# An fp32 attention block on one core: every engine's instructions in the order of the program, with sums, weight splits and weighting at other places in it

## The chip, the core and the metric

The kernel runs on one core of one Trainium2 chip. A core has five engines that each work through a list of instructions of their own: TensorE (PE, matrix products into the banks of PSUM), VectorE (DVE), ScalarE (ACT), GpSimd (POOL) and SyncE (SP, which here only issues loads). An instruction starts when the one before it on its engine has been issued and the semaphores that it waits for have been raised, so what stands ahead of it in its engine's list can hold it up, whether or not the two have anything to do with each other. The metric is the device time of one execution in microseconds (us), as the median of several runs.

## The reference

The reference is a two-layer decoder trunk in fp32 on a sequence of 512 tokens with a model width of 1024: a recurrent layer with its feed-forward block, and an attention layer with its own. The change touches the attention layer alone:

```python
def dilated_attention_mixer(h, w_q, q_norm, w_o, k, v, cos, sin):
    q = (h @ w_q).reshape(B, S, N_GROUPS, Q_HEADS, HEAD_DIM)    # 3 groups, 8 heads of 128
    q = rms_norm(q, q_norm[:, None, :])
    q = apply_partial_rope(q, cos, sin)                         # turns the first 32 of 128 elements
    q = q.reshape(B, S, N_GROUPS, KV_HEADS, Q_PER_KV, HEAD_DIM)
    for g, (window, dilation) in enumerate(DILATION_GROUPS):    # (128, 1), (512, 4), (2048, 16)
        o, l = dilated_window_attention(q[:, :, g], k[:, :, g], v[:, :, g], window, dilation)
    ...
    wts = jax.nn.softmax(jnp.stack(lses, axis=0), axis=0)       # the groups weighted by their sums
    o = jnp.sum(wts[..., None] * jnp.stack(outs, axis=0), axis=0)
    return o.reshape(B, S, Q_HEADS * HEAD_DIM) @ w_o
```

The two weightings together are one softmax over the keys of all three groups, and so the kernel computes it.

## The kernel before, in words

The activations lie transposed, as 8 blocks of 128 features by 512 tokens. A product in fp32 is made of three products in a faster format: each operand x is split into a rounded part hi and a rest lo = x - hi, and PE forms hi·hi, lo·hi and hi·lo (`mm3`, L163 to L165; in the projections L1048 to L1050).

**The weights** come in pieces of 128x1024 through `Stream` (L70 to L153): SP loads a piece into one of two raw buffers `wr`, and two pieces ahead of its use it is split into `wh` and `wl`, of which there are three buffers each. For most pieces ACT copies hi (L117) and DVE subtracts (L124). For pieces of kind "dma", those of the query and output projections among them, ACT copies hi, ACT writes the negated weight into lo (L120), and POOL issues a DMA that adds to it (L121).

**The query passes** (`project`, L1030) take one group of keys (g = 0, 1, 2) and one half of the heads (kv = 0, 1) each: 16 steps of 6 matmuls, four weight pieces by four tiles of 128 tokens. In the last piece each step completes one tile of queries for four heads, and `collect` (L971) follows it up: DVE applies the gain out of the bank (`kn`, L982), ACT squares the bank in place (L984), DVE sums the squares (L985) and rotates (`rotate`, four small operations, L994 to L997). After the last tile, `normed` gives DVE the `factors` (L1006 and eight operations of `rsqrt`, L261 to L270, some 0.2 us each) and one `scale` of a tile per step (L1014). A given number of steps later, the lag, PE transposes each tile (`turn`, L1127), and ACT copies the result out (`qt`, L1129). A call `at(n, fn)` puts such work off by n steps; `tick` counts them. `tick` comes straight after `done` in the same step, so that `at(1, ...)` falls due at once.

**The attention** (`attend`) goes through 32 units: 2 halves kv by 4 blocks n of 128 tokens by 4 phases p. For a unit u, `scores` forms three products in one bank, normally bank S, of which there is one. `softmax` then has DVE add the masks and find the least (two operations, L1192 and L1195), ACT take the exponential (L1200), DVE the reciprocal (L1201) and POOL the multiplication with it (L1202). Three units later `turned` transposes the weights (L1214) and `halve` splits them into `ph` (ACT, L279) and `pl` (DVE, L280); after every second unit, `values` multiplies them with the values. `query_parts` splits the queries of the next block n into `qh` (ACT) and `ql` (DVE), three each. At the end of the first half, `move` splits four tiles of the output `o_t` by `halve`.

**What fills the gaps.** While `attend` runs, `plan` inserts the steps of the second half's query passes (groups 0 and 1 as passes of four tiles, group 2 as an early and a late pass of two tiles) and then those of the first half of the output projection. The second half of that projection, and the second feed-forward block, follow.

**What sets the order.** In the attention, the framework's scheduler decides how the instructions of each engine are ordered: it goes by its own model of when each is ready, and takes weight splits, the softmax and the splits of `turned` first, since these stand under `high_priority`. The feed-forward blocks stand under `manual_schedule` for all five engines, which keeps the order in which the program issues.

Of the kernel before, what the change touches and what calls it, by code (L numbers as in the profile page):

```python
# [73 lines left out]
class Stream:  # L74


    def __init__(self, tc, nc, pool, pieces, ahead_load, ahead_split):
# [4 lines left out]
        self.hold, self.gate = {}, {}  # L82

# [22 lines left out]
    def _split(self, i):  # L106
# [8 lines left out]
        def do(c):  # L115
            with self.tc.high_priority():
                nc.scalar.copy(hi[:, c], r[:, c])  # L117
                kind = self.pieces[i][1]
                if kind == "dma":
                    nc.scalar.mul(lo[:, c], r[:, c], -1.0)  # L120
                    nc.gpsimd.dma_start(lo[:, c], self.pieces[i][0][:, c], accum_op=ALU.add)  # L121
                else:
# [34 lines left out]
def trunk(tc, A, out):  # L157
    nc = tc.nc
# [58 lines left out]
    p_q = add_pieces([A["w_q"][i] for i in (*range(24), *range(20, 24))], "dma")  # L217
# [725 lines left out]
def attention(tc, A, ap, ws, env):  # L943
# [30 lines left out]
    def collect(raw, nh, j, n, st, tab, g_row):  # L974
# [10 lines left out]
        V.tensor_reduce(st["sq"][:, j], rows.rearrange("q (i d) -> q i d", i=nh), mybir.AxisListType.X, ALU.add)  # L985
        st["kn"].append(dst)
        at(1, lambda: rotate(x, nh, tab))
# [11 lines left out]
    def normed(st, nh, tab, turn, lag, tiles=range(4)):  # L999
# [16 lines left out]
        at(1, factors)  # L1016
        for j, t in enumerate(tiles):
            at(2 + j, lambda t=t: scale(t))
            at(lag + j, lambda t=t: turn(t, kn[t]))
# [96 lines left out]
    def project_q(kv):  # L1116
# [3 lines left out]
        for j, (g, tiles) in enumerate(passes):  # L1120
            def done_q(t, ps, g=g, st={}, tiles=tiles, j=j):
                collect(ps, 4, t - tiles[0], len(tiles), st, t, 3 + g)
                if t == tiles[-1]:
# [10 lines left out]
                    normed(st, 4, 0, turn, {3: 7}.get(j, 8), tiles)  # L1134

            yield from project(p_q + 12 * kv + 4 * j, xh, xl, done_q, tiles)

    def first(fn):

        def run(*args):  # L1140
            with tc.high_priority():
                return fn(*args)
        return run

# [13 lines left out]
    def query_parts(kv, n):  # L1158
        for g in range(3):
            if (kv, n, g) not in qs_:  # L1160
                query_part(kv, n, g)

    def scores(kv, n, p):
# [20 lines left out]
        softmax(n, p, ps, pr, mn, g0, w, nb)  # L1184
        prs[kv, n, p] = pr
        if n < 3 and p == (2 if kv else 3) or not kv and p == 3 and (0, 1, 2) in qt:
            query_parts(kv + n // 3, (n + 1) % 4)

    @first
    def softmax(n, p, ps, pr, mn, g0, w, nb):  # L1190
# [8 lines left out]
        den = ap.tile([128, 1], F32, name="den", bufs=4)  # L1199
        S.activation(pr[:, :width], pr[:, :width], AF.Exp, bias=mn[:, 1:2], scale=-1.0, accum_out=den)  # L1200
        V.reciprocal(den, den)  # L1201
        G.tensor_scalar(pr[:, :width], pr[:, :width], den, None, ALU.mult)  # L1202
# [5 lines left out]
    def turned(kv, n, p):  # L1208
# [10 lines left out]
        first(halve)(pt.rearrange("q (b k) -> q b k", k=128)[:, :nb], ph[:, :nb, p % 2], pl[:, :nb, p % 2])  # L1219

    def values(kv, n, p):
# [23 lines left out]
        else:  # L1245
            halve(src, *(x[:, 4 * kv:4 * kv + 4, ns].rearrange("q h (p i) -> q h p i", p=4)
                         for x in (env["xhs"], env["xls"])))

    def attend():
# [3 lines left out]
        for u in range(32 + LAG):  # L1253
            if u >= LAG:
                turned(*units[u - LAG])
            yield u + 0.4
            if u < 32:
# [29 lines left out]

    drain(project_q(0))
# [96 lines left out]
```

## Time and profile before

| what | value |
|---|---|
| median of 3 runs | 1165.84 us (1165.73 to 1167.09) |
| profiled execution, its own time | 1166.22 us |
| its span in the trace | 1164.4 us |
| PE busy | 1151.9 us, 99% of the span |
| DVE busy | 851.5 us, 73% |
| ACT busy | 623.8 us, 54% |
| POOL busy | 186.3 us, 16% |

By the places of its lines in the trace, the keys and values are projected until about 577 us, the first half's query passes run until about 645, the attention with all that fills it until about 798, the rest of the output projection until 828, and the second feed-forward block to the end. A busy time counts each instruction from its start to its end as the profiler models it; instructions of one engine overlap at their ends. A matmul of 512 columns is shown as 0.39 us long, while the next one starts about 0.23 us behind it, so a PE that is 99% busy may still have waited, and the stalls have to be read from the starts and from the waits.

### The profile page before, as it was taken

The numbers are of one execution on the slowest core, as the hardware profiler recorded it, in microseconds if no ns is written. First come the engines' busy times: TensorE is split into PE (matmuls) and PEld (weight loads), VectorE is DVE, ScalarE is ACT, GpSimd is POOL, SyncE is SP. The second block draws the span as 40 slices with busy tenths as digits, with TensorE's granted clock in tenths as the row PEclk, the third lists the DMA queues.
The fourth block names the chain that finished last, engine by engine and source line by source line (L and its number), as shares of the span: only waits on it lengthen the run. The fifth ranks groups of instructions, "written<-read, shape, count | busy, mean of one in ns | idle before, by whom it ended". The sixth has DMA issues, their size and how long they took to land.

```text
span 1164.4 us, 15128 instructions
## 1 busy us (share of the span) xinstructions
PE 1151.9 (99%) x5403; PEld 952.2 (82%) x5403; DVE 851.5 (73%) x1525; ACT 623.8 (54%) x901; POOL 186.3 (16%) x221
## 2 busy tenths in 40 slices
PE   9999999999999999999999999999999999999998
PEld 6788888888888888888888888798888888888887
DVE  7988688968777676887565667765988777676864
ACT  6797455543435353565555667665555435353532
POOL 4210010201011000020411334341002011011000
PEclk9999999999999999999999999999999999999999
DMA  7643366966665723433978657534668665757323
GB/s 244 149 114 110 105 225 159 242 193 160 183 164 174 188 73 82 129 107 89 222 182 178 142 113 179 127 73 108 219 160 233 186 165 177 182 162 191 81 71 128
DMA packets 92234, 179.61 MB, mean 154 GB/s; under 512 B 8704, under 2 KB 27008, under 8 KB 92160
## 3 DMA queue, kind: packets, MB, share of 16 engines
q1 hardware_dynamic: 72720, 130.80, 34.6%
q0 software_dynamic: 18864, 47.19, 22.9%
q8 instruction: 43, 0.70, 0.2%
q10 hardware_dynamic: 576, 0.66, 0.2%
q14 instruction: 31, 0.25, 0.1%
HBM read 164.99 MB, written 2.10 MB: 143 GB/s over the span
## 4 chain that ended last, share of the span: by engine, by line
PE 92%; DVE 3%; ACT 2%; issue 1%; DMA 1%; POOL 0%; ACTq 0%; DVEq 0%; SPq 0%
PE ps L165 25%; PE ps L164 25%; PE ps L163 25%; PE ps L1048 5%; PE ps L1049 5%; PE ps L1050 5%; PE ps L1127 1%; PE ps L1214 1%; DVE xc L451 1%; DMA h<-in_x 0%; ACT pr L1200 0%; PE ps L296 0%; DVE ql L280 0%; ACT wh L117 0%; DMA wr<-in_w_in 0%
## 5 line engine op out<-in xcount | busy, mean ns | idle before, releaser
L117 ACT CAST wh<-wr 128x1024 fp32r<-128x1024 f32 (+2 forms) x136 | 131.2, 969 | 136.3 <-PE ps L164 83.1
L164 PE MATMUL ps<-wl,xh 128*128 128x512 f32 x320 | 124.7, 390 | 0.0
L165 PE MATMUL ps<-wh,xl 128*128 128x512 f32 x320 | 124.7, 390 | 0.0
L163 PE MATMUL ps<-wh,xh 128*128 128x512 f32 x320 | 124.7, 390 | 0.0
L165 PE MATMUL ps<-gh,wl 128*128 128x512 f32 x288 | 114.6, 398 | 0.3
L163 PE MATMUL ps<-gh,wh 128*128 128x512 f32 x288 | 113.8, 395 | 0.0
L164 PE MATMUL ps<-gl,wh 128*128 128x512 f32 x288 | 113.7, 395 | 0.0
L124 DVE TENSOR_TENSOR wl<-wr,wh 128x1024 fp32r<-128x1024 f32 (+2 forms) x93 | 100.0, 1083 | 17.4 <-ACT wh L117 17.0
L649 POOL DMA_DIRECT2D S<-in_f_in x40 | 48.2, 1237 | 370.8 <-DMA S<-in_f_in 187.2
L163 PE MATMUL ps<-xh,wh 128*128 128x512 f32 x256 | 101.1, 396 | 0.7 <-ACT xh L274 0.7
L663 ACT CAST wh<-S 128x1024 fp32r<-128x1024 f32 x60 | 63.0, 1050 | 70.4 <-PE ps L165 28.0
L164 PE MATMUL ps<-xl,wh 128*128 128x512 f32 x256 | 100.2, 391 | 0.1
L165 PE MATMUL ps<-xh,wl 128*128 128x512 f32 x256 | 100.0, 391 | 0.0
L664 DVE TENSOR_TENSOR wl<-S,wh 128x1024 fp32r<-128x1024 f32 x60 | 73.2, 1222 | 31.5 <-ACT wh L663 31.5
L163 PE MATMUL ps<-wh,T 128*128 128x512 f32 x240 | 93.6, 390 | 0.0
L165 PE MATMUL ps<-wh,T 128*128 128x512 f32 x240 | 93.6, 390 | 0.0
L164 PE MATMUL ps<-wl,T 128*128 128x512 f32 x240 | 93.5, 390 | 0.0
L1048 PE MATMUL ps<-wh,xh 128*128 128x512 f32 x224 | 91.6, 409 | 0.0
L1050 PE MATMUL ps<-wh,xl 128*128 128x512 f32 x224 | 87.8, 392 | 0.0
L1049 PE MATMUL ps<-wl,xh 128*128 128x512 f32 x224 | 87.4, 390 | 0.0
L781 DVE TENSOR_TENSOR h<-h,ps 128x512 f32<-128x512 f32 x64 | 43.3, 685 | 54.9 <-PE ps L165 54.9
L163 PEld LDWEIGHTS ps<-wh,xh 128*128 128x128 f32 x320 | 60.1, 188 | 12.6
(284 smaller groups left out, 2669.7 us busy)
## 6 DMA issues: line engine op xcount, KB each, us to landing
S<-in_f_in SPq DMA_DIRECT2D x40, 512.0 KB, 6.4
S<-in_f_in POOLq DMA_DIRECT2D x40, 512.0 KB, 8.9
wr<-in_f_out SPq DMA_DIRECT2D x36, 512.0 KB, 5.2
wr<-in_w_q SPq DMA_DIRECT2D x28, 512.0 KB, 6.9
wl<-in_w_q POOLq DMA_DIRECT2D x28, 512.0 KB, 7.6
GA<-in_f_in SPq DMA_DIRECT2D x20, 512.0 KB, 4.9
GB<-in_f_in SPq DMA_DIRECT2D x20, 512.0 KB, 6.9
UB<-in_f_in SPq DMA_DIRECT2D x20, 512.0 KB, 4.9
```

Of the source, the lines that this page charges most:

```text
L117: nc.scalar.copy(hi[:, c], r[:, c])
L124: a = eng.tensor_tensor(lo[:, c], r[:, c], hi[:, c].bitcast(F32), ALU.subtract)
L163: PE.matmul(ps, wh, xh, start=first, stop=False, skip_group_check=on)
L164: PE.matmul(ps, wh, xl, start=False, stop=False, skip_group_check=on)
L165: PE.matmul(ps, wl, xh, start=False, stop=last, skip_group_check=on)
L649: nc.gpsimd.dma_start(c, p.part(1, q, n == "S1", i), accum_op=ALU.add)
L663: S.copy(hi, r)
L664: V.tensor_tensor(lo, r, hi.bitcast(F32), ALU.subtract)
L781: V.tensor_tensor(by_time(x), by_time(x), in_turn(ps), ALU.subtract)
L1048: PE.matmul(ps[t], xh[k][:, r], wh[:, c], start=k == 0, stop=False)
L1049: PE.matmul(ps[t], xh[k][:, r], wl[:, c], start=False, stop=False)
L1050: PE.matmul(ps[t], xl[k][:, r], wh[:, c], start=False, stop=k == 7)
```

## The change

1. From the first query pass to the end of the first half of the output projection, all five engines stand under `manual_schedule`; the `high_priority` of softmax and of the splits in `turned` is gone.
2. In that stretch `lo_first` has ACT write the negated weight ahead of hi, so that the accumulating DMA is issued earlier, and `al` asks for raw pieces four ahead rather than two.
3. Of the first twelve query pieces every second one is split by DVE (L124) and not by the DMA.
4. The sum of squares is issued with the rotation, in `at(1, ...)`; factors and scales come one step later; the lags become 8 for passes of four tiles and 6 for those of two.
5. `weigh` (reciprocal and multiplication) and the subtractions for `pl`, and for the split of the attention's output, go into a list `put_off`, which `catch_up` empties in the next unit, just ahead of that unit's `scores`. The first group's query split is issued ahead of the exponential, the other two behind it.

```diff
+        self.lo_first = False
...
             with self.tc.high_priority():
-                nc.scalar.copy(hi[:, c], r[:, c])
                 kind = self.pieces[i][1]
+                if kind != "dma" or not self.lo_first:
+                    nc.scalar.copy(hi[:, c], r[:, c])
                 if kind == "dma":
                     nc.scalar.mul(lo[:, c], r[:, c], -1.0)
                     nc.gpsimd.dma_start(lo[:, c], self.pieces[i][0][:, c], accum_op=ALU.add)
+                    if self.lo_first:
+                        nc.scalar.copy(hi[:, c], r[:, c])
...
-    p_q = add_pieces([A["w_q"][i] for i in (*range(24), *range(20, 24))], "dma")
+    p_q = add_pieces([A["w_q"][i] for i in range(12)], "dma", 2)
+    add_pieces([A["w_q"][i] for i in (*range(12, 24), *range(20, 24))], "dma")
...
         S.activation(rows, rows, AF.Square)
-        V.tensor_reduce(st["sq"][:, j], rows.rearrange("q (i d) -> q i d", i=nh), mybir.AxisListType.X, ALU.add)
+        sums = st["sq"][:, j]
+
+        def reduce():
+            V.tensor_reduce(sums, rows.rearrange("q (i d) -> q i d", i=nh), mybir.AxisListType.X, ALU.add)
+
         st["kn"].append(dst)
-        at(1, lambda: rotate(x, nh, tab))
+        if nh == 2:
+            reduce()
+            at(1, lambda: rotate(x, nh, tab))
+        else:
+            at(1, lambda: (reduce(), rotate(x, nh, tab)))
...
-        at(1, factors)
+        wait = 1 if nh == 2 else 2
+        at(wait, factors)
         for j, t in enumerate(tiles):
-            at(2 + j, lambda t=t: scale(t))
+            at(wait + 1 + j, lambda t=t: scale(t))
             at(lag + j, lambda t=t: turn(t, kn[t]))
...
-                    normed(st, 4, 0, turn, {3: 7}.get(j, 8), tiles)
+                    normed(st, 4, 0, turn, 8 if len(tiles) == 4 else 6, tiles)
...
-        softmax(n, p, ps, pr, mn, g0, w, nb)
+        lowest(n, p, ps, pr, mn, g0, w, nb)
         prs[kv, n, p] = pr
-        if n < 3 and p == (2 if kv else 3) or not kv and p == 3 and (0, 1, 2) in qt:
-            query_parts(kv + n // 3, (n + 1) % 4)
+        groups = ()
+        if n < 3 and p == (2 if kv else 3) or not kv and n == p == 3 and (0, 1, 2) in qt:
+            groups = range(3)
+        query_parts(kv + n // 3, (n + 1) % 4, groups[:1])
+        width = g0 + 2 * w
+        den = ap.tile([128, 1], F32, name="den", bufs=4)
+        S.activation(pr[:, :width], pr[:, :width], AF.Exp, bias=mn[:, 1:2], scale=-1.0, accum_out=den)
+        query_parts(kv + n // 3, (n + 1) % 4, groups[1:])
+
+        def weigh():
+            V.reciprocal(den, den)
+            G.tensor_scalar(pr[:, :width], pr[:, :width], den, None, ALU.mult)
+
+        put_off.append(weigh)
+
+    put_off = []
+
+    def catch_up():
+        while put_off:
+            put_off.pop(0)()
...
-        first(halve)(pt.rearrange("q (b k) -> q b k", k=128)[:, :nb], ph[:, :nb, p % 2], pl[:, :nb, p % 2])
+        parts(pt.rearrange("q (b k) -> q b k", k=128)[:, :nb], ph[:, :nb, p % 2], pl[:, :nb, p % 2])
+
+    def parts(src, hi, lo):
+        S.copy(hi, src)
+        put_off.append(lambda: V.tensor_tensor(lo, src, hi.bitcast(F32), ALU.subtract))
...
             yield u + 0.4
+            catch_up()
             if u < 32:
                 scores(*units[u])
...
+    manual = tc.manual_schedule(engines={E.PE, E.DVE, E.Activation, E.SP, E.Pool})
+    manual.__enter__()
+    ws.lo_first, ws.al = True, 4
     drain(project_q(0))
...
     drain(o0)
-    ws.asp = 1
+    catch_up()
+    ws.asp, ws.al, ws.lo_first = 1, 2, False
+    manual.__exit__(None, None, None)
```

On SP the order is the same row by row. On PE the transposes of the turns stand elsewhere at four places and a few matmuls have changed places with their neighbours; DVE and ACT are reordered throughout. Three places of the program are shown. The number behind a name tells one buffer's use from the next; it differs a little between the two programs.

**DVE, the first units of the attention (kv = 0, n = 0), while the third query pass of the first half is followed up.** `ps` with `grow` is the gain of a finished tile, `ps` with `ssum` and with `far` are the two mask operations of a unit. Before, from the third tile on:

```order
L982 TENSOR_TENSOR kn_5622<-ps_5430,grow_1855 128x512
L1192 ISA pr_5642,mn_5643<-ps_5632,ssum_78 128x128
L1192 ISA mn_5643 128x1
L994 TENSOR_TENSOR ra_5626<-kn_5622,cc_1862 128x128
L1195 ISA pr_5642,mn_5643<-ps_5632,far_1853,mn_5643 128x128
L1195 ISA mn_5643 128x1
L985 TENSOR_REDUCE sqc_5571<-ps_5430 128x4
L995 TENSOR_TENSOR rbt_5627<-kn_5622,ss_1863 128x4x16
```

Now, from the third tile on:

```order
L987 TENSOR_TENSOR kn_5620<-ps_5429,grow_1855 128x512
L993 TENSOR_REDUCE sqc_5569<-ps_5429 128x4
L1007 TENSOR_TENSOR ra_5624<-kn_5620,cc_1862 128x128
L1008 TENSOR_TENSOR rbt_5625<-kn_5620,ss_1863 128x4x16
L1009 TENSOR_TENSOR rbt_5625<-kn_5620,ss_1863 128x4x16
L1010 TENSOR_TENSOR kn_5620<-ra_5624,rbt_5625 128x4x32
L1202 RECIPROCAL den_5596<-den_5596 128x1
L1215 ISA pr_5642,mn_5643<-ps_5632,ssum_78 128x128
L1215 ISA mn_5643 128x1
L1218 ISA pr_5642,mn_5643<-ps_5632,far_1853,mn_5643 128x128
```

The sum now stands directly behind the gain of its own tile, with nothing between them, the rotation behind the sum, and the mask operations of the unit behind the whole tile. Where the mask operations of unit 2 stood behind one gain, they now stand behind two whole tiles, that of the second and that of the third.

**ACT, the first tile of the second half's pass for group 1.** Before:

```order
L120 ACTIVATE wl157_5999<-wr157_5996 128x1024
L117 CAST wh157_5998<-wr157_5996 128x1024
L1200 ACTIVATE pr_5988,den_5992<-pr_5988,mn_5989 128x512
L984 ACTIVATE ps_5692<-ps_5692 128x512
L984 ACTIVATE ps_5730<-ps_5730 128x512
```

Now:

```order
L1198 ACTIVATE pr_5988,den_5992<-pr_5988,mn_5989 128x512
L122 ACTIVATE wl157_5997<-wr157_5774 128x1024
L125 CAST wh157_5996<-wr157_5774 128x1024
L989 ACTIVATE ps_5688<-ps_5688 128x512
L989 ACTIVATE ps_5727<-ps_5727 128x512
```

The two passes over a weight piece, which stood ahead of the exponential, now stand between it and the square of the first tile.

**DVE, the end of the follow-up in the same pass.** Before, the subtraction `pl` stands ahead of the factors (the row of `epsv` is their first):

```order
L997 TENSOR_TENSOR kn_6097<-ra_6101,rbt_6102 128x4x32
L280 TENSOR_TENSOR pl_6054<-ps_6119,ph_6053 128x3x128
L1201 RECIPROCAL den_6087<-den_6087 128x1
L985 TENSOR_REDUCE sqc_6009<-ps_5769 128x4
L1192 ISA pr_6150,mn_6151<-ps_6140,ssum_78 128x256
L1192 ISA mn_6151 128x1
L1006 SCALAR_TENSOR_TENSOR sqc_6009<-sqc_6009,epsv_4010 128x16
```

Now, from the first of the factors:

```order
L1019 SCALAR_TENSOR_TENSOR sqc_6007<-sqc_6007,epsv_4010 128x16
L266 TENSOR_SCALAR qr4y_6106<-sqc_6007 128x16
L269 TENSOR_TENSOR qr4a_6107<-qr4y_6106,sqc_6007 128x16
L270 SCALAR_TENSOR_TENSOR qr4a_6107<-qr4a_6107,qr4y_6106 128x16
L271 SCALAR_TENSOR_TENSOR qr4y_6106<-qr4a_6107,qr4y_6106 128x16
L272 SCALAR_TENSOR_TENSOR qr4a_6107<-qr4y_6106,sqc_6007 128x16
L273 TENSOR_TENSOR qr4a_6107<-qr4a_6107,qr4y_6106 128x16
L274 SCALAR_TENSOR_TENSOR qr4a_6107<-qr4a_6107 128x16
L275 SCALAR_TENSOR_TENSOR qr4y_6106<-qr4a_6107,qr4y_6106 128x16
L1027 TENSOR_TENSOR kn_6008<-kn_6008,qr4y_6106 128x512
L1202 RECIPROCAL den_6087<-den_6087 128x1
L1242 TENSOR_TENSOR pl_6052<-ps_6116,ph_6051 128x3x128
```

The subtraction for which `values` waits has moved behind the nine operations of the factors and one scale; before, it stood ahead of them.

More of the change, by code (lines that the diff above doesn't have):

```diff
@@ L1132, in turn @@
                             query_part(0, 0, g)
-                    normed(st, 4, 0, turn, {3: 7}.get(j, 8), tiles)
+                    normed(st, 4, 0, turn, 8 if len(tiles) == 4 else 6, tiles)
             yield from project(p_q + 12 * kv + 4 * j, xh, xl, done_q, tiles)
[L1138 to L1143, printed above, removed]
     o_t = ap.tile([128, 4, 384], F32, name="o_t", bufs=1)
@@ L1156, in query_part, with query_parts @@
         qs_[kv, n, g] = qh, ql
-    def query_parts(kv, n):
-        for g in range(3):
+    def query_parts(kv, n, groups=range(3)):
+        for g in groups:
             if (kv, n, g) not in qs_:
@@ L1183, in scores, with lowest @@
         mn = ap.tile([128, 2], F32, name="mn", bufs=4)
-        softmax(n, p, ps, pr, mn, g0, w, nb)
+        lowest(n, p, ps, pr, mn, g0, w, nb)
         prs[kv, n, p] = pr
-        if n < 3 and p == (2 if kv else 3) or not kv and p == 3 and (0, 1, 2) in qt:
-            query_parts(kv + n // 3, (n + 1) % 4)
-    @first
-    def softmax(n, p, ps, pr, mn, g0, w, nb):
+        groups = ()
[14 more added lines that the diff above has]
+            put_off.pop(0)()
+    def lowest(n, p, ps, pr, mn, g0, w, nb):
         width = g0 + 2 * w
@@ L1198, in softmax @@
             far[:, 0:2 * nb, f0:f0 + 64], 1.0, mn[:, 0:1], ALU.add, ALU.min, mn[:, 1:2])
[L1199 to L1202, printed above, removed]
     def blocks(n, p):
@@ L1245, in values @@
         else:
-            halve(src, *(x[:, 4 * kv:4 * kv + 4, ns].rearrange("q h (p i) -> q h p i", p=4)
+            parts(src, *(x[:, 4 * kv:4 * kv + 4, ns].rearrange("q h (p i) -> q h p i", p=4)
                          for x in (env["xhs"], env["xls"])))
@@ L1285, in move @@
             halve(o_t[:, i, :], xh[i][:, 0:384], xl[i][:, 0:384])
+    E = mybir.EngineType
+    manual = tc.manual_schedule(engines={E.PE, E.DVE, E.Activation, E.SP, E.Pool})
+    manual.__enter__()
+    ws.lo_first, ws.al = True, 4
     drain(project_q(0))
```

## The prediction

> **What bounds the kernel now.** I read the busy time and the chain first, then the windows of the stretch that the change covers, then what PE waits for there. On the page, busy time by engine and the chain that ended last:
>
> ```profile
> PE 1151.9 (99%) x5403; PEld 952.2 (82%) x5403; DVE 851.5 (73%) x1525; ACT 623.8 (54%) x901; POOL 186.3 (16%) x221
> PE 92%; DVE 3%; ACT 2%; issue 1%; DMA 1%; POOL 0%; ACTq 0%; DVEq 0%; SPq 0%
> ```
>
> PE is the bound, and the change takes no matmul away. It can gain only what PE waits in the stretch from 577 to 798 us, and lose whatever other engines deliver later than PE asks for it. Two windows of the attention (start:end and length; sum and busy time with counts of PE, weight load, DVE, ACT, POOL; clock, DMA share, GB/s):
>
> ```profile
> 645.00:700.00 55.00, 54.44 (x325) 47.29 (x325) 38.73 (x140) 36.20 (x66) 19.35 (x17) 1.00 0.57 128
> 700.00:735.00 35.00, 32.27 (x214) 28.33 (x213) 25.44 (x75) 27.82 (x48) 14.66 (x11) 1.00 0.77 175
> ```
>
> Here DVE is busy 70 and 73%, ACT 66 and 79%: each has room on average, but little, so that the order within a few microseconds decides. What PE waits for from 640 to 800 us (sum, count, longest):
>
> ```profile
> PE ps L1127 <- ACT qt L1129: 1.3, 2, 1.0
> PE ps L165 <- DVE ql L280: 1.3, 2, 0.7
> PE ps L163 <- ACT qt L1129: 1.2, 1, 1.2
> PE ps L163 <- DVE mn L1195: 0.5, 1, 0.5
> PE ps L164 <- DVE pl L280: 0.3, 1, 0.3
> ```
>
> That is 4.6 us, and it is the gain that is there to be had; by the gaps between matmul starts I make it at most 7. The question is what the new order makes late.
>
> **Prices.** Grouped rows of the stretch, first DVE's weight split, then sum, ACT's two weight passes, the query split and its copy out, DVE's half of it, and one of the four splits of `move` (busy, mean ns):
>
> ```profile
> L124 DVE TENSOR_TENSOR wl<-wr,wh 128x1024 fp32r<-128x1024 f32 x3 | 3.7, 1223 | 0.2 <-ACT wh L117 0.2
> L985 DVE TENSOR_REDUCE sqc<-ps 128x4 f32<-128x512 f32 x20 | 13.7, 685 | 1.1 <-ACT ps L984 1.1
> L120 ACT ACTIVATE wl<-wr 128x1024 fp32r<-128x1024 f32 x9 | 9.5, 1059 | 3.1 <-PE ps L1049 3.0
> L117 ACT CAST wh<-wr 128x1024 fp32r<-128x1024 f32 x9 | 9.3, 1034 | 0.0
> L279 ACT CAST qh<-qt 128x512 fp32r<-128x512 f32 x9 | 5.1, 619 | 1.0 <-PE ps L164 1.0
> L1129 ACT COPY qt<-ps 128x512 f32<-128x512 f32 x8 | 4.6, 578 | 3.1 <-PE ps L1127 3.0
> L280 DVE TENSOR_TENSOR ql<-qt,qh 128x512 fp32r<-128x512 f32 x9 | 6.1, 684 | 2.0 <-ACT qh L279 2.0
> L279 ACT CAST xh<-o_t 128x384 fp32r<-128x384 f32 x4 | 2.0, 513 | 0.0
> ```
>
> The sum's row tells most: 20 sums wait only 1.1 us for their squares, since DVE does other work meanwhile. The timeline shows how long a square takes, and how close operations follow each other:
>
> ```profile
> 649.42 0.69 DVE L982 TENSOR_TENSOR kn<-ps,grow 128x512 f32<-128x512 f32 x1 [2.35 <-PE ps L1050]
> 650.14 0.58 ACT L984 ACTIVATE ps<-ps 128x512 f32<-128x512 f32 x1 [0.32 <-DVE kn L982]
> 650.14 0.29 DVE L994 TENSOR_TENSOR ra<-kn,cc 128x128 f32<-128x128 f32 x1
> 650.95 0.28 DVE L1192 CUSTOM_DVE_ANT_0 pr<-ps,ssum 128x128 f32<-128x128 f32 x1
> 653.73 0.68 DVE L985 TENSOR_REDUCE sqc<-ps 128x4 f32<-128x512 f32 x1
> 654.33 0.67 DVE L982 TENSOR_TENSOR kn<-ps,grow 128x512 f32<-128x512 f32 x1
> 654.93 0.27 DVE L1192 CUSTOM_DVE_ANT_0 pr<-ps,ssum 128x128 f32<-128x128 f32 x1
> 585.52 0.17 DVE L1006 SCALAR_TENSOR_TENSOR sqc<-sqc,epsv 128x16 f32<-128x16 f32 x1
> 587.51 2.50 DVE L1014 TENSOR_TENSOR kn<-kn,qr4y 128x512 f32<-128x512 f32 x4
> 684.59 0.42 DVE L1192 CUSTOM_DVE_ANT_0 pr<-ps,ssum 128x256 f32<-128x256 f32 x1 [1.21 <-PE ps L165]
> 685.06 0.48 DVE L1195 CUSTOM_DVE_ANT_1 pr<-ps,far,mn 128x256 f32<-128x256 f32 x1
> 685.64 0.73 ACT L1200 ACTIVATE pr<-pr,mn 128x512 f32<-128x512 f32 x1 [0.38 <-DVE mn L1195]
> ```
>
> From gain to rotation stand 0.72 us, the rotation takes 0.81 (650.14 to 650.95), a sum 0.60 and a gain without a wait 0.60. The square ends at 650.72, 1.30 us after its gain began; I put the sum's start at 1.33. In the new order nothing stands between them, so a tile costs DVE 1.33 + 0.60 + 0.81 = 2.75 us, 0.73 of it waiting. If the square were always done in time it would be 2.01; that is the lower end, and the upper one has an ACT operation of 1.03 to 1.06 ahead of the square. I take 2.75, as in the row, since the square cannot start before the gain has read the bank. A tile leaves PE every 1.36 us or so (6 matmuls of 0.23). The factors take 587.51 - 585.52 = 2.0 us with a small wait, 1.9 without; a scale 0.63; the mask pair about 0.95 (684.59 to 685.54), some 0.7 for unit widths of 128.
>
> **The change part by part.** Each place is a walk along DVE's or ACT's new order from an event of before, up to the moment at which PE asked.
>
> *First half, passes 1 and 2.* The first gain, and the last matmul ahead of the turn, then the turn:
>
> ```profile
> 577.45 0.69 DVE L982 TENSOR_TENSOR kn<-ps,grow 128x512 f32<-128x512 f32 x1 [1.79 <-PE ps L1050]
> 590.65 0.40 PE L1050 MATMUL ps<-wh,xl 128*128 128x512 f32 x1
> 590.88 0.60 PE L1127 MATMUL ps<-ident,kn 128*128 128x128 f32 x4
> ```
>
> From 577.45: 0.45 for an ACT pass that holds up the first square, four tiles at 2.75, the split of a weight piece that now stands ahead of the factors (1.22), factors 1.9, first scale 0.7: 592.7, where PE asks at 590.9. That is 1.8; pass 2, with the same walk less the 0.45, 1.4; pass 3 turns inside the attention. **+3.2**. With 2.01 a tile it would be 0.
>
> *Units n = 0.* The third scores of the attention and the query split that ends a wait of 0.7:
>
> ```profile
> 656.97 0.22 PE L163 MATMUL ps<-kh,qh 128*128 128x128 f32 x1
> 661.93 0.69 DVE L280 TENSOR_TENSOR ql<-qt,qh 128x512 fp32r<-128x512 f32 x1
> ```
>
> First gain at 649.42, tile through at 652.2, mask pair of unit 1 at 652.95; then two whole tiles (5.5) and the pair of unit 2 (0.7): bank S is free at 659.15, and PE wants it for unit 3 at 656.97, 2.2 late. Behind it a fourth tile (2.75), factors (1.9), scale (0.6), reciprocal and `pl` (0.35), the pair of unit 3 (0.7): 665.4; then three `ql` of 0.6: 667.2 against 662.67 (the last of these rows and its 0.7). **+4.5**; with 2.01 a tile, 2.3.
>
> *Second half, group 1.* Scores and values of two units:
>
> ```profile
> 694.28 0.35 PE L163 MATMUL ps<-kh,qh 128*128 128x256 f32 x1
> 696.77 0.28 PE L163 MATMUL ps<-ph,vh 128*128 128x256 f32 x1
> ```
>
> ACT now does exponential (685.64 to 686.4 with its accumulator), two weight passes (2.0), square: the first sum starts at 689.0. The rest of that tile (1.4), two more (5.5), `pl` (0.5) and mask pair (0.95) end at 697.4; PE wants the bank at 694.28: 3.1. A fourth tile (2.75), factors, scale, `pl` (0.5): 703.1; PE wants that `pl` 0.1 behind 696.77 + 3.1: 3.2. The turns stand behind weight passes on ACT: 1.5 by the same walk. Sum 7.8, less what PE waits there today (the L1127 rows, and some that the waits do not list: 2.3). **+5.5**; 2.5 at 2.01 a tile.
>
> *Early pass of group 2.*
>
> ```profile
> 714.73 0.69 DVE L982 TENSOR_TENSOR kn<-ps,grow 128x512 f32<-128x512 f32 x1
> 718.75 0.28 PE L163 MATMUL ps<-kh,qh 128*128 128x256 f32 x1
> 721.14 0.28 PE L163 MATMUL ps<-ph,vh 128*128 128x256 f32 x1
> ```
>
> A tile (2.75), `pl` (0.6) and mask pair (0.95) from 714.73 and with their hand-overs end at 719.6: 0.9 late. A second tile, factors, scale, `pl`: 725.5, where PE, 0.9 late, asks at 722.1: 3.3. **+4.2**; at 2.01, 2.7.
>
> *Change of halves.* All on ACT in one row now: mask pair 0.95, exponential 0.9, weight passes 2.1, two copies out 1.2, four splits of `move` 2.05, `ph` 0.5, three `qh` 1.9, and DVE's `ql` 0.7: 10.2, with two hand-overs 10.6. PE's matmuls between the scores of the last unit and those of the next half come to 4.8 us, each taken with its usual distance to the next: 5.8, less 1.5 that it waits there today (1.2 of it listed). **+4.3**; 3 if operations overlap as elsewhere.
>
> *The rest.* The late pass of two tiles comes out even by the same walk: 2.4 against 2.3. SP's order does not change, and of raw buffers there are two, so "four ahead" is worth 0. Six accumulating DMAs less, and POOL's multiplication later, lie under POOL's 84% idle time: 0; uncovered, a later multiplication would delay the transposes three units on, some 10 us away. Past 798 us nothing differs: 0.
>
> Sum: 3.2 + 4.5 + 5.5 + 4.2 + 4.3 = 21.7. The profiled execution took 1166.2 us, 0.4 more than the median. 1166.2 + 21.7 = 1187.9, and 1187.5 against the median. With every lower end it is 0 + 2.3 + 2.5 + 2.7 + 3 = 10.5, so 1176; with an ACT pass ahead of half of the 16 tiles concerned, +8 to +12, about 1200.
>
> **Rivals.**
>
> *A, faster.* The order of the program lets every engine take what PE needs next, and the five waits go: 1161, or 1159 with what the waits do not list. For it speaks DVE's idle quarter. It needs DVE not to wait for squares: at 2.01 a tile the walks still leave 10 us, so the gains would also have to be asked for later than today. Point of decision: mask pairs end ahead of 656.97 and 694.28.
>
> *B, no change.* The stalls move from `qt` and `ql` to the mask pairs and cost what they cost today, since a PE that is delayed by 2 us asks for everything behind it 2 us later, and one stall pays for the next. I have counted so within a place; if it holds between places too, and tiles cost 2.01, it is 1165 to 1168.
>
> *C, slower still.* [...] The chip's clock is 1.00 in both windows above, where no stall is longer than 1.4 us; at the head of the program, behind idle time, matmuls of the same width run slower:
>
> ```profile
> 1.45 4.02 PE L346 MATMUL ps<-warm 128*128 128x512 bf16 x9 [1.45 <-DVE warm L343]
> ```
>
> Nine in 4.02 us are about 0.43 each, twice the 0.23 of later. If each of four stalls (3.1, 3.2, 3.3, 5.8) costs some 3.7 us at half pace, so 1.8 us each, it is 7 more: 1195. [...]
>
> **How the numbers follow.** The forecast 1187 has 0.66 (1176 to 1200 its own range), C 0.12, A 0.13, B 0.09. The range is to leave out no more than A and the top of C: 1163 to 1201. Against a measurement that tells about 0.2% (2.3 us) from no change: faster 0.13, same 0.09, slower 0.78.
>
> **What would show it.** In the profile of the changed kernel: the sum's group waits for ACT some 0.7 us in each of about 20 tiles (14 us, against 1.1); PE waits for the mask operations by 2 to 3 us at two places, for `pl` by 3 at two, for `ql` by about 5 at the change of halves; the windows lose PE time there and nowhere after 798. If sums wait but PE does not, the walks have the wrong moment at which PE asks, and the forecast falls to B. If PE's waits are each under 1 us, A holds. If the clock falls under 1.00, C does.

## The result

The changed kernel takes 1217.57 us (median of 4 runs, 1208.35 to 1218.52), the kernel before 1166.32 us beside it: a ratio of 1.0421 with an interval of 1.037 to 1.0472, so 51 us slower. The direction was forecast, the size was not: 1217.6 lies above the range of 1163 to 1201. Busy time by engine, the chain and the clock in 40 slices, from the page of the changed kernel:

```profile
PE 1177.2 (97%) x5403; PEld 968.9 (80%) x5403; DVE 860.4 (71%) x1531; ACT 616.8 (51%) x895; POOL 180.4 (15%) x215
PEclk9999999999999999999999888899999999999999
PE 85%; DVE 8%; ACT 3%; issue 2%; DMA 1%; POOL 1%; ACTq 0%; DVEq 0%; POOLq 0%
```

The matmuls are the same 5403, and DVE and ACT have 11% of the chain where they had 5%. New is the second row: the clock granted to PE falls in four slices, which it did nowhere before. Three windows of the attention (columns as in the prediction; the clock is the third number from the end):

```profile
645.00:700.00 55.00, 50.35 (x274) 42.62 (x275) 26.49 (x94) 29.53 (x54) 13.29 (x14) 0.94 0.51 115
700.00:750.00 50.00, 40.27 (x224) 34.63 (x223) 29.66 (x99) 25.71 (x44) 16.30 (x13) 0.85 0.58 127
750.00:800.00 50.00, 40.45 (x203) 34.94 (x201) 23.79 (x78) 24.62 (x49) 11.43 (x11) 0.77 0.39 85
```

From 645 to 700 us PE issues 274 matmuls where it issued 325, and it is slowed as well as idle. What PE waits for from 570 to 870 us, and the row of the sums among DVE's groups:

```profile
PE ps L168 <- DVE pl L1242: 7.5, 5, 3.1
PE ps L167 <- DVE mn L1218: 7.4, 4, 2.9
PE ps L1141 <- DVE kn L1027: 3.0, 2, 1.7
PE ps L167 <- ACT qh L284: 2.9, 1, 2.9
PE ps L168 <- DVE xl L1242: 2.9, 1, 2.9
PE ps L1063 <- DMA wl<-in_w_q: 1.7, 1, 1.7
L993 DVE TENSOR_REDUCE sqc<-ps 128x4 f32<-128x512 f32 x24 | 16.6, 692 | 19.5 <-ACT ps L989 19.5
```

The sums wait 19.5 us in 24 tiles, 0.8 each, where 20 of them waited 1.1 before. Where the long stalls lie, in the timeline of PE (start, duration, and in brackets the wait):

```profile
664.25 0.30 PE L167 MATMUL ps<-kh,qh 128*128 128x128 f32 x1 [1.92 <-DVE mn L1218]
670.47 0.55 PE L167 MATMUL ps<-kh,qh 128*128 128x256 f32 x1 [2.00 <-DVE mn L1218]
709.57 0.36 PE L167 MATMUL ps<-kh,qh 128*128 128x256 f32 x1 [2.92 <-DVE mn L1218]
715.40 0.58 PE L168 MATMUL ps<-pl,vh 128*128 128x256 f32 x1 [2.38 <-DVE pl L1242]
745.62 0.58 PE L168 MATMUL ps<-pl,vh 128*128 128x256 f32 x1 [3.15 <-DVE pl L1242]
760.94 0.33 PE L167 MATMUL ps<-kh,qh 128*128 128x128 f32 x1 [2.89 <-ACT qh L284]
787.08 0.80 PE L168 MATMUL ps<-xl,wh 128*128 128x512 f32 x1 [2.86 <-DVE xl L1242]
```

The trace's own records of the clock give the stretches at half speed (start and length in us; the end of the program left out):

```
670.43  6.83      711.39 10.24      745.53 10.24
762.59  6.83      786.49 10.24      841.10  3.41
```

All lengths are multiples of 3.41 us, and so, within 0.02, are the distances between the starts (711.39 - 670.43 is 12 times 3.413). So the decision seems to be made on a fixed grid; I call one stretch of it a cell.

**An account by starts.** For each matmul from 570 to 880 us I took the distance to the next start and subtracted the median distance for its width (0.227 us for 512 columns, 0.12 for 256, 0.11 for 128). In a stretch at half clock, up to one more such distance is put down to the clock; the rest of an excess over 0.25 us is a stall. In us, with the table's kernels explained below:

| kernel | span | stalls | clock | smaller excess | at half clock, stretches |
|---|---|---|---|---|---|
| before | 1164.4 | 6.7 | 0 | 2.8 | 0 |
| changed | 1216.6 | 37.6 | 19.5 | 4.5 | 47.8, 6 |
| changed, second trace | 1213.7 | 39.9 | 13.1 | 4.4 | 34.1, 6 |
| all edits but the fixed order | 1165.5 | 5.9 | 0 | 4.1 | 0 |
| fixed order alone | 1237.9 | 50.8 | 25.6 | 6.5 | 64.9, 12 |
| sums a step later | 1204.7 | 27.0 | 17.5 | 3.7 | 41.0, 6 |
| fixed order on PE and SP alone | 1175.4 | 11.7 | 5.5 | 3.4 | 13.7, 2 |
| fixed order on DVE, ACT, POOL alone | 1196.5 | 26.0 | 9.2 | 5.9 | 23.9, 3 |
| three repairs | 1198.8 | 25.7 | 13.2 | 4.2 | 34.1, 6 |

The span grew by 52.2 us, and the account gives 30.9 of stalls, 19.5 of clock and 1.7 of smaller excess. So there are two things to test: where the stalls come from, and whether the slow clock is a cost of its own or only lies in time that PE would wait anyway.

### The profile page after: what moved, and what is told of

It is laid out like the page before. It is cut to its first block, busy times and chain, and to the rows that moved or that the text cites. A ratio compares the mean times of both kernels' runs of the same rounds, so it can differ in the third digit from the quotient of the medians.

```text
span 1216.6 us, 15135 instructions
## 1 busy us (share of the span) xinstructions
PE 1177.2 (97%) x5403; PEld 968.9 (80%) x5403; DVE 860.4 (71%) x1531; ACT 616.8 (51%) x895; POOL 180.4 (15%) x215
## 4 chain that ended last, share of the span: by engine, by line
PE 85%; DVE 8%; ACT 3%; issue 2%; DMA 1%; POOL 1%; ACTq 0%; DVEq 0%; POOLq 0%
PE ps L169 24%; PE ps L168 24%; PE ps L167 23%; PE ps L1062 4%; PE ps L1063 4%; PE ps L1064 4%; DVE sqc L993 1%; ACT ps L989 1%; PE ps L1141 1%; ACT pr L1198 1%; DVE kn L987 1%; PE ps L1233 1%; DMA wl<-in_w_q 1%; DVE xc L456 0%; DVE pl L1242 0%
## 5 line engine op out<-in xcount | busy, mean ns | idle before, releaser
L120 ACT CAST wh<-wr 128x1024 fp32r<-128x1024 f32 (+2 forms) x109 | 103.2, 954 | 139.6 <-PE ps L168 80.1
L167 PE MATMUL ps<-wh,xh 128*128 128x512 f32 x320 | 124.5, 389 | 0.0
L128 DVE TENSOR_TENSOR wl<-wr,wh 128x1024 fp32r<-128x1024 f32 (+2 forms) x99 | 107.2, 1091 | 23.6 <-ACT wh L120 23.4
L669 DVE TENSOR_TENSOR wl<-S,wh 128x1024 fp32r<-128x1024 f32 x60 | 73.2, 1222 | 31.5 <-ACT wh L668 31.5
L1062 PE MATMUL ps<-wh,xh 128*128 128x512 f32 x224 | 94.3, 421 | 0.0
```

The lines of the kernel that those rows point to most:

```text
L128: a = eng.tensor_tensor(lo[:, c], r[:, c], hi[:, c].bitcast(F32), ALU.subtract)
L167: PE.matmul(ps, wh, xh, start=first, stop=False, skip_group_check=on)
L669: V.tensor_tensor(lo, r, hi.bitcast(F32), ALU.subtract)
L1062: PE.matmul(ps[t], xh[k][:, r], wh[:, c], start=k == 0, stop=False)
```

## The experiments

**All edits but the fixed order.**

```diff
-    manual = tc.manual_schedule(engines={E.PE, E.DVE, E.Activation, E.SP, E.Pool})
-    manual.__enter__()
...
-    manual.__exit__(None, None, None)
```

> The changed kernel with every edit but the manual schedule: the framework's scheduler orders all five engines again, from the changed program. Theory (the fixed order is what puts DVE's and ACT's work behind what it waits for): the stalls of 2 to 3 us go, and with them the stretches at half clock; 1164 to 1170. Rival (the put-off sums, weighting and splits are late in themselves, whoever orders them): PE still waits 2 us or more for mask operations, pl or xl at several places, and the time stays above 1190.

1167.56 us (10 runs), ratio 1.0009 (0.9999 to 1.0018). The longest of PE's waits:

```profile
PE ps L1141 <- ACT qt L1143: 2.1, 4, 1.0
PE ps L167 <- ACT ph L1241: 1.0, 2, 0.6
```

The theory holds. With the put-offs, the new lags, lo ahead of hi and the DVE splits in place, but the scheduler in charge, the time is that of before within what can be measured. The 51 us need the fixed order.

**The fixed order alone**, added to the kernel before by the same lines.

> The kernel before with nothing but the manual schedule added over the same stretch: nothing is put off. Theory (a fixed order alone costs, and the put-offs repair a part of it): slower than the changed kernel, 1225 to 1250, since subtractions and reciprocals then stand on DVE directly behind the ACT operation that they wait for. Rival (the put-offs are the cause): 1170 to 1195.

1239.72 us (one run). Its waits begin with

```profile
PE ps L1049 <- DMA wl<-in_w_q: 16.4, 4, 4.7
PE ps L164 <- DVE pl L280: 7.9, 5, 3.6
PE ps L163 <- DVE mn L1195: 5.6, 2, 2.9
```

The time is as the theory said: the fixed order costs 73 us on the program as it was, and the other edits win back 22 of them. The reason given there, subtractions and reciprocals behind what they wait for, is only a part of it: PE waits longest for the accumulating DMAs (16.4 us, 1.7 in the changed kernel).

**Sums a real step later.**

```diff
-            at(1, lambda: (reduce(), rotate(x, nh, tab)))
+            at(2, lambda: (reduce(), rotate(x, nh, tab)))
```

> The changed kernel with the sum and the rotation of a tile put off by one real step, so that the next tile's gain stands between a gain and its sum. Theory of the prediction (DVE's wait of 0.73 us for each square carries half of the stalls): a tile costs 2.0 us of DVE instead of 2.75, the stalls of 2.1, 2.1 and 3.1 at the mask operations shrink to under 1.5, half of the drops in the clock go; 1185 to 1200. Rival (what ACT has ahead of the squares, and pl behind the factors, carry them): 1210 to 1220, as the changed kernel.

1205.87 us (4 runs), ratio 1.0337 (1.0322 to 1.0353). The sums' row, and the longest of PE's waits:

```profile
L993 DVE TENSOR_REDUCE sqc<-ps 128x4 f32<-128x512 f32 x24 | 16.4, 683 | 3.3 <-ACT ps L989 3.3
PE ps L168 <- DVE pl L1242: 7.5, 5, 3.3
PE ps L167 <- ACT qh L284: 3.0, 2, 2.9
PE ps L168 <- DVE xl L1242: 2.9, 1, 2.9
PE ps L167 <- DVE mn L1218: 2.4, 1, 2.4
```

The mechanism is shown: one step moves the sums' wait from 19.5 to 3.3 us, PE's wait for the mask operations from 7.4 to 2.4, and the waits of the first passes' turns for `kn` (3.0) are gone from the list. The size is less than expected: 11.7 us, to 1206 and not 1200, since PE waits for `pl`, `qh` and `xl` as long as before, and all six stretches at half clock remain, where half of them were to go.

**The clock by itself.** Ten stalls in the second feed-forward block of the kernel before, where PE does not wait otherwise, made by ACT between two matmuls into one bank:

```diff
+                    if kk and p is p_f2 and n in ("S2", "UB"):
+                        for _ in range(probes.pop(0)):      # 4, 5, 6, 7, 8, 6, 7, 5, 8, 6
+                            S.copy(ps[1], ps[1])
```

> The kernel before with ten stalls put into PE's work of the second feed-forward block, where PE otherwise never waits: ACT copies a bank onto itself 4 to 8 times between two matmuls that add to it, which should hold PE up for about 1.4, 1.9, 2.4, 2.9 and 3.4 us, two stalls of each length some 16 us apart or more. Theory G (the clock is decided on a fixed grid of 3.41 us, by PE's share of work in one cell): stalls of 1.4 and 1.9 never drop the clock, 3.4 mostly does, and 2.4 and 2.9 do so or not, depending on where they fall in a cell. [...] Each drop lasts 3.4 to 10.2 us at half clock, by the changed kernel's trace, and costs up to half of that.

1219.95 us (one run). The stalls came out longer than intended. Five of them waited for 3.59 to 5.97 us, each with a whole cell in which no matmul ran, and all five dropped the clock, as theory G has it. So the other five decide, the first, second, sixth, eighth and tenth; in PE's timeline:

```profile
873.57 0.50 PE L163 MATMUL ps<-wh,T 128*128 128x512 f32 x1 [1.79 <-ACT ps L751]
899.76 0.50 PE L163 MATMUL ps<-wh,xh 128*128 128x512 f32 x1 [2.39 <-ACT ps L751]
1044.21 0.50 PE L163 MATMUL ps<-wh,xh 128*128 128x512 f32 x1 [2.99 <-ACT ps L751]
1116.04 0.50 PE L163 MATMUL ps<-wh,xh 128*128 128x512 f32 x1 [2.39 <-ACT ps L751]
1173.53 0.50 PE L163 MATMUL ps<-wh,xh 128*128 128x512 f32 x1 [2.99 <-ACT ps L751]
```

The eight stretches begin at 874.88, 926.08, 970.46, 997.76, 1045.55, 1072.86, 1117.23 and 1144.54. So a stall of 2.39 dropped the clock once and once not, one of 2.99 once and once not, and one of 1.79 did. The cells of that grid in which those five stalls lie, for the last one both over which it stretches (start:end and length, then sum and busy time of PE, and the rest as above):

```profile
871.47:874.88 3.41, 1.62 (x8) 1.10 (x7) 0.67 (x2) 2.91 (x5) 0.05 (x1) 1.00 0.88 298
895.36:898.78 3.42, 2.01 (x9) 1.32 (x8) 3.37 (x5) 3.10 (x6) 0.00 (x0) 1.00 1.10 258
1042.14:1045.55 3.41, 1.34 (x6) 1.13 (x7) 0.40 (x1) 2.88 (x5) 0.00 (x0) 1.00 0.25 95
1113.82:1117.23 3.41, 1.19 (x5) 1.02 (x6) 0.25 (x1) 3.03 (x5) 0.00 (x0) 1.00 0.35 135
1168.43:1171.84 3.41, 2.11 (x10) 1.41 (x8) 3.41 (x5) 3.10 (x6) 0.00 (x0) 1.00 0.00 0
1171.84:1175.26 3.42, 1.73 (x8) 1.43 (x9) 0.85 (x2) 2.53 (x4) 0.00 (x0) 1.00 0.57 153
```

Where PE was busy for 1.62 us of a cell or less, the next cell ran at half clock; at 1.73 or more it did not. That is theory G, but with a bound near half a cell of 3.41 us, which it did not have: by its text stalls of 1.9 us or less never drop the clock, and one of 1.79 did, since it fell inside one cell (871.47 to 874.88). The length of a stall alone does not decide: of two of 2.39 us one dropped the clock and one did not. In this block, of 512-column matmuls back to back, a stretch lasted one cell or two (3.41 or 6.83 us); in the attention of the changed kernel up to three (10.24), and with the fixed order on DVE, ACT and POOL alone once five (17.07).

**The changed kernel again**, unaltered.

> The changed kernel once more, unaltered, for a second trace. If the clock is decided on a grid that runs free of the program, the stalls of the first trace come back within 0.3 us each up to the first drop, while the drops begin at other stalls or last for another number of cells of 3.41 us: the time lies anywhere from 1205 to 1220. If a stall's own length decides, the same stalls drop the clock as in the first trace (the ones of 2.2, 3.1, 3.3, 3.1 and 3.1 us), and the time is 1217 to 1219.

1215.74 us (one run). Every stall over 1 us is there again, within 0.6 us of its length and most within 0.1, but the stretches at half clock begin at 674.77, 715.73, 746.45, 760.10, 784.00 and 845.44 and last 34.1 us together, not 47.8. The first begins 3.0 us behind its stall, where it began with it. The stall of 3.1 us at the scores of unit 10, which had a stretch 1.8 us behind it, now has none: it ends at 710.38 and spreads over two cells, the first busy for 1.98 us and the second for 1.94. The stretch at 715.73 belongs to the next stall, which fills most of the cell ahead of it:

```profile
708.90:712.32 3.42, 1.94 (x13) 1.83 (x14) 2.56 (x9) 1.99 (x5) 1.55 (x1) 1.00 0.00 0
712.32:715.73 3.41, 0.83 (x5) 0.42 (x3) 3.07 (x17) 1.61 (x2) 0.89 (x1) 1.00 0.23 40
```

That is what the first expectation said, and it speaks against the second. The program's work is the same, its place on the grid is not; that the spread of the four runs, 1208 to 1218.5 us, comes from this too fits their mean clocks (0.98 to 0.99), but is not shown run by run.

**PE kept at work in its stalls.** Matmuls whose results are overwritten stand ahead of the one that waits:

```diff
+    def busy(n, po=None):
+        po = bank("O") if po is None else po
+        for _ in range(n):
+            PE.matmul(po[:, 256:512], vh[0][:, 0, 0:128], kh[0][0][:, 0:256], start=True, stop=True)
...
+        if (kv, n, p) in ((0, 0, 3), (0, 1, 0), (1, 0, 0)):
+            busy({(0, 0, 3): 16, (0, 1, 0): 16, (1, 0, 0): 24}[kv, n, p])
+        elif (kv, n, p) == (0, 2, 2):
+            busy(24, pos_[0])
```

and likewise repeats of the first matmul of three `values` (20, 24, 10 times) and of the output projection (12).

> The changed kernel with PE kept at work where it stalls: matmuls whose results are overwritten (16 to 24 of 256 columns, 12 of 512; at the scores of units 3, 4, 10 and 16, at the values of units 7, 11 and 15, and at the head of the output projection) stand ahead of the matmul that has to wait, 1.2 to 3.0 us in each place. They do not make anything ready sooner, so PE's useful work waits as long as before. Theory (a part of the loss is PE's clock, which falls where PE is idle for too much of a cell of 3.41 us): most of the stretches at half clock go, and 10 to 20 us with them: 1198 to 1208. Rival (the stretches at half clock lie in time that PE would wait out anyway, and cost next to nothing): 1214 to 1222.

1208.84 us (4 runs), ratio 1.0367 (1.0351 to 1.0383), 8.7 us under the changed kernel with more work for PE. One stretch of 6.83 us at half clock is left. The windows over the same part:

```profile
645.00:700.00 55.00, 51.85 (x307) 44.52 (x307) 26.47 (x94) 29.88 (x55) 13.29 (x14) 1.00 0.53 120
700.00:750.00 50.00, 47.31 (x317) 41.64 (x315) 31.28 (x104) 28.34 (x49) 16.51 (x14) 1.00 0.59 127
750.00:800.00 50.00, 44.57 (x274) 38.57 (x275) 28.87 (x94) 25.41 (x54) 13.67 (x13) 0.93 0.39 85
```

The clock is a cost of its own: the rival's 1214 to 1222 is out, though the theory's own 1198 to 1208 is missed by a little. By the account, 16.8 us of clock went; in their place stand 18.8 us of filling matmuls (134 by 0.12 and 12 by 0.227), 14.4 us less of stalls, and 1.2 more of small excess. So the filling was 4.4 us longer than the stalls that it covered, and by the account the kernel kept about 11 us of the 16.8 (the spans of the two traces differ by 10.2). All of that is against the first trace; the second had only 13.1 us of clock to give. One of the changed kernel's own runs, that with the highest mean clock (0.99), took 1208.35 us, as little as these; the others took 1215.7 to 1218.5. So the 8.7 us are uncertain by a few.

**The subtraction `pl` ahead of the factors.**

```diff
                 given[i] += 1
+                catch_up()
```

> The changed kernel with the put-off list emptied after every inserted step of a query pass or projection, too: the subtraction pl then stands ahead of the factors that come with a later step. Theory of the prediction (pl behind factors and scale makes the values wait): the stalls of 2.7 and 3.3 us at pl fall under 1.5 each, and with them the two drops in the clock that follow; 1203 to 1212. Rival (the wait moves on to the mask operations or the turns behind it): within 4 us of 1217.6.

1217.72 us (4 runs): the rival. The stall at the values of unit 7 falls from 2.7 to 1.5, but that of unit 11 stays (3.7, was 3.3), the turns wait up to 1.9 instead, and as many stretches at half clock remain, for 47.8 us. The list that is emptied earlier holds the weighting and `xl` too, so more than one subtraction moved, and the wait moved with them.

**Three repairs together**: the two above, and `move` two steps later.

```diff
-                if i == 1 and given[i] == steps:
+                if i == 2 and given[i] == 2:
                     move()
```

> Three repairs together in the changed kernel: the sum a real step later, the put-off list emptied after every inserted step, and the four splits of the change of halves issued two steps of the late pass later. Theory (each place has its own cause in the order, so that the repairs add up): the stalls at mask operations, pl and qh shrink to 1.5 us or less, those of xl and of the last units stay, and one or two drops of the clock are left; 1183 to 1196. Rival (DVE and ACT are simply too full there for any fixed order of this program, so that repairs only move the stalls): above 1198.

1200.13 us (4 runs), ratio 1.0285 (1.0269 to 1.03). The rival's side of the line, just: the three repairs bring 17.4 us, 5.7 more than the sums alone. What remains:

```profile
PE ps L168 <- DVE pl L1242: 7.7, 5, 3.3
PE ps L168 <- DVE xl L1242: 2.8, 1, 2.8
```

The change of halves went from a stall of 3.1 us for `qh` to one of 1.4. For `pl` PE waits as long as ever: in DVE's timeline the sum and rotation of a tile, all factors and a scale (700.92 to 704.93) still stand directly ahead of the one that ends the longest of these waits. The rival's reason, that DVE and ACT are too full for any fixed order, is not shown by this: only orders of this one program were tried.

**The fixed order on some engines.** PE and SP alone:

```diff
-    manual = tc.manual_schedule(engines={E.PE, E.DVE, E.Activation, E.SP, E.Pool})
+    manual = tc.manual_schedule(engines={E.PE, E.SP})
```

> The changed kernel with the fixed order on PE and SP alone: the scheduler orders DVE, ACT and POOL. Theory (it is DVE's and ACT's fixed order that makes things late; PE's own order hardly changed): 1164 to 1172, and no PE stall above 1.5 us. Rival (PE itself, held to the order of the program, cannot pass over a matmul that is not ready): stalls of 2 us and more remain and the time is above 1185.

1176.98 us (4 runs), ratio 1.0086 (1.0071 to 1.0101), between the two. Its longest waits:

```profile
PE ps L1141 <- ACT qt L1143: 5.3, 4, 2.6
PE ps L167 <- ACT qh L284: 2.4, 1, 2.4
```

DVE, ordered by the scheduler, is hardly late any more (0.9 us for `pl`); the fixed order of PE and SP costs 10 us, at transposes and scores that wait for ACT, about half of it as lost clock (5.5). And on DVE, ACT and POOL alone:

> The changed kernel with the fixed order on DVE, ACT and POOL alone; the scheduler orders PE and SP. Theory (what DVE and ACT deliver late is late whatever PE's order is, as PE's order hardly changes): 1200 to 1220. Rival (a scheduled PE finds other work for the stalls): under 1190.

1198.53 us (one run), just under the theory's range and 8.5 us above the rival's. The theory's reason does not hold: a scheduled PE no longer waits for mask operations, and other waits come up:

```profile
PE ps L1063 <- DMA wl<-in_w_q: 7.8, 4, 4.8
PE ps L1233 <- POOL pr L1203: 5.7, 4, 1.8
```

So the larger part of the loss comes with the fixed order of DVE, ACT and POOL (32 us with PE and SP free, 10 with these two alone fixed, 51 together).

**Two stalls that the prediction did not have.** The subtraction for `xl` at once (`halve` for `parts` in `values`):

> The changed kernel with the subtraction for xl (the split of the attention's output) issued at once again, not put off by a unit. Theory (it is the put-off that makes the head of the output projection wait 3.1 us for xl, a stall that the prediction did not have): that stall falls under 1 us, and the drop of the clock with it; the other stalls stay within 0.3 us, and the time is 4 to 8 us under the changed kernel's, 1208 to 1213. Rival (DVE is behind with other work there, whatever stands in the list): the stall stays above 2 us.

and hi ahead of lo again (`ws.lo_first` left False):

> The changed kernel with hi written ahead of lo again. In the fixed order the accumulating DMA is then issued an ACT pass (1.0 us) later. Theory (the stall of 1.9 us for a DMA into wl, which the prediction did not have, is a DMA issued too late): it grows to about 2.9 us, and other pieces begin to wait as well; 1217 to 1230. Rival (DMAs have room enough): no stall for a DMA grows by more than 0.3 us.

With `xl` at once, 1215.41 us (one run), and the stall at the head of the output projection is 3.08 us: the rival. The list is not to blame. The timeline of DVE in the changed kernel shows what is:

```profile
781.86 0.68 DVE L987 TENSOR_TENSOR kn<-ps,grow 128x512 f32<-128x512 f32 x1
783.19 0.69 DVE L993 TENSOR_REDUCE sqc<-ps 128x4 f32<-128x512 f32 x1 [0.65 <-ACT ps L989]
784.60 0.16 DVE L1019 SCALAR_TENSOR_TENSOR sqc<-sqc,epsv 128x8 f32<-128x8 f32 x1
786.36 0.67 DVE L1242 TENSOR_TENSOR xl<-ps,xh 128x512 fp32r<-128x512 f32 x1
```

A tile and all factors of the late pass, 4.5 us, stand ahead of `xl`, for which PE waits from 784 on. With `xl` at once they still do, from 781.52 to 785.94. With hi first, 1213.66 us (one run): the DMA stall grew from 1.95 to 3.19 us, as the theory said, and now drops the clock too, but no other piece waits for its DMA, and the whole is not slower, since the mask operations that were late at 670.47 no longer are. Its 1217 to 1230 is missed.

**What the kernel before has left.** The copy `qt` first for the scheduler, and then the query split too:

```diff
+                        with tc.high_priority():
+                            S.copy(q, pt.rearrange("q (h p i) -> q p h i", h=4, p=4))
```

> The kernel before with one line more: the copy out of a turned tile (qt) is taken first by the scheduler, as weight splits are. In the trace of before PE waits 2.5 us in all for that copy, behind weight passes on ACT. Theory (the copy then goes ahead of a weight pass of 1 us): the waits at the turns shrink to 1 us in all; 1164 to 1165.5. Rival (a weight pass that is put back makes something else late, or the scheduler's order changes elsewhere too): within 0.1% of before, or slower.

> The kernel before with the copy qt and both halves of the query split taken first by the scheduler. PE still waits 1.3 us for ql and 1.2 for qt with the copy alone. Theory (what is left of PE's waits in the attention is work that the scheduler puts behind weight passes): 1163.5 to 1165, faster than before by 0.1 to 0.25%. Rival (what is put first pushes back something else that PE needs): as before within 0.1%, or slower.

1165.63 us, ratio 0.9992 (0.9983 to 1.0001), and 1166.11 us, ratio 0.9999 (0.9990 to 1.0008), of 11 runs each. Neither is told apart from before: the rival both times. In the first the turns wait 0.5 us for `qt`, where it was 1.3, and the other waits stay, so that PE's listed waits come to 4.0 us, where they were 4.6. In the second `ql` is gone from the list, but the wait for `pl` grew from 0.3 to 1.2, and the sum is 4.0 again. A gain of under 1 us, if there is one, these runs cannot tell.

## Why the prediction was wrong

*Direction and mechanism: right.* DVE in the fixed order pays the wait for each square. The prediction had 1.33 us from gain to sum; the trace has 781.86 to 783.19, 1.33, and with that wait gone the first passes no longer waited and the mask operations waited 2.4 us instead of 7.4, near to its lower walk. Gross stalls by place, forecast and measured:

| place | forecast | measured (second trace) |
|---|---|---|
| passes 1 and 2 | 1.8, 1.4 | 1.88, 1.41 (1.86, 1.40) |
| scores of unit 3 | 2.2 | 2.08 (2.08) |
| the next, given as `ql` | 3.0 | 2.17 (2.17), for the mask operations, at the scores of unit 4 |
| scores of unit 10, values of unit 7 | 3.1, 3.2 | 3.09, 2.68 (3.08, 3.22) |
| turns of group 1 | 1.5 | 0.84 (0.84) |
| early pass, scores and values | 0.9, 3.3 | 0.77, 3.31 (0.77, 3.30) |
| change of halves | 5.8 | 4.0 (5.1): 3.05 and 0.97, in the second also 1.18 |

In two rows PE waited for another product than the forecast had: at unit 4 for the mask operations and not for `ql`, and at the change of halves mostly for `qh` (2.9 us) and little for `ql` (0.8). That the sizes come near there is in part luck.

*The sum: failed.* It had the clock at nothing, and some 9 us of stalls too few. Of the 30 us by which the time lies above the forecast, the clock is the larger part (19.5 us in the first trace, 13.1 in the second). Of the stalls: "Comes out even ... 2.4 against 2.3" was wrong. From the values of unit 15 to the end of the stretch the stalls of more than 0.6 us add up to 10.6 (1.55, 3.14, 0.84, 0.62, 0.88, 0.61, 0.87, 0.62 and 1.42), some 8 more than before. For 3.1 of them the walk left out that `xl` stands behind the late pass's factors as `pl` does behind the others; the rest are waits of up to 1.6 us for `pl`, `vl`, `vh`, `ph` and `qt`, several of them in units behind that pass, for which the prediction has no term. "Worth 0" for the weight pieces was wrong too: a DMA into `wl` comes 1.95 us late at 645.64, where before had no such wait. These two come to some 10 us; the places of the table stay 4 us under their forecast (22.2 of 26.2), and waits under 0.6 us bring about 3 back. That makes the 9 us between the forecast's 21.7 us of stalls and the 30.9 measured.

*Rival C: right in kind, mis-sized, and not in the forecast.* It had 1.8 us for each of four stalls, 7 in all, by the time that nine matmuls take at the head of the program: no run shows that price for a stall, it was an estimate of mine. Measured are 13 to 20 us of lost clock over six stretches (19.5 in the first trace, 13.1 in the second, so 3.3 and 2.2 a stretch), for two reasons that the probe and the two traces show. Half a cell of idle time can be enough: in the probe 1.62 us of work in a cell of 3.41 dropped the clock. So stalls of 2 us count (that of 2.00 at 670.47 has a stretch with it), and not only the four from 3.1 us on that it took, while one of 2.99 in the probe and one of 3.1 in the second trace dropped nothing. And a stretch can last longer than one cell: in the first trace five of six lasted two or three, 6.83 to 10.24 us. Its 1195 was still 22 us short. The walk's own sum with the measured price of the clock, 1187.5 + 13 to 20, would have been 1200 to 1208, and with the rest 1210 to 1217.

*A and B: out.* None of the five waits went, though those for `ql` (1.3 to 0.8) and for `qt` at the scores (1.2 to 0.5) became shorter; PE's for `pl` and the mask operations are 14.9 us where they were 0.8.

## What to carry to other kernels

An order that a scheduler found from its own model is not bound to improve when the order in which the program happens to be written is fixed instead: here the fixed order alone took 73 us more than the scheduler's, on the same operations. Before fixing it, walk each engine's list with the time at which PE asks for each product, every place to the end of the stretch, and look above all for an operation that waits on another engine directly ahead of one that PE needs. Then price a stall not by its length alone, but with what it may do to PE's clock: here a cell of 3.41 us in which a stall left PE 1.62 us of work dropped the clock in the probe, a stall of 2.00 us in the changed kernel had 6.83 us at half clock with it, and that kernel's stretches lasted one to three cells (3.41 to 10.24 us).

## What was not expected of the hardware

Whether a stall drops PE's clock depends on where it falls on a grid that does not move with the program: stalls of 2.39 and of 2.99 us did it once and once not, and in two traces of the changed kernel the first stretch begins at 670.43 and at 674.77, 4.34 us apart, which is no multiple of 3.413. For the probe's 512-column matmuls the bound lies between 1.62 and 1.73 us of busy time in 3.41. In the attention it is less sharp. Three cells of the changed kernel, the first and the last before a drop, and a fourth, before a drop in its second trace,

```profile
667.02:670.43 3.41, 1.46 (x7) 0.84 (x5) 3.10 (x16) 1.07 (x3) 1.65 (x2) 1.00 0.52 76
776.25:779.66 3.41, 1.93 (x12) 1.27 (x10) 2.93 (x12) 1.56 (x4) 1.07 (x2) 1.00 0.70 120
837.69:841.10 3.41, 2.35 (x18) 2.03 (x18) 1.35 (x3) 0.77 (x3) 1.56 (x1) 1.00 0.00 0
671.36:674.77 3.41, 2.41 (x11) 1.78 (x12) 2.83 (x7) 1.90 (x5) 0.36 (x1) 1.00 1.01 267
```

show a drop after 1.46 us and none after 1.93, but one after 2.35 and one after 2.41. In the cell busy for 2.35 us all 17 matmuls that start there (838.51 to 841.02) have 128 or 256 columns, where those of the probe have 512. With hi ahead of lo again, a cell busy for 1.57 us (742.66 to 746.07) had no drop behind it. What such narrower matmuls count for on the grid stays open.
